# Low-rank update on one core: ScalarE's spreads as hardware loops, GpSimd narrowing whole groups, one wait a turn on VectorE

## The chip, the core and the metric

The kernel runs on one core of a Trainium2 chip. The core has five engines with an instruction stream each: PE (TensorE, matrix products), DVE (VectorE), ACT (ScalarE), POOL (GpSimd) and SP (SyncE), which here only issues transfers. They share a scratch memory of 128 partitions (SBUF). PE writes its products into PSUM. Sixteen DMA engines move data between the chip's memory (DRAM) and SBUF. The engines synchronise by semaphores: an instruction can wait until a semaphore has reached a value, and add to one when it is done.

The metric is the device time of one execution in microseconds. The kernel before takes 123.73 us, the median of three runs from 123.73 to 123.92.

## The reference

```python
batch, seq, d_model, r = 16, 512, 768, 16
lora = np.matmul(np.matmul(x, A), B)        # A is 768 x 16, B is 16 x 768
return (x + scale * lora).astype(np.float32)
```

`x` has 8192 rows of 768 floats, 25.2 MB, and the result has the same size. The inner matrices are small: per row 16 numbers `y = x A` are made, and from those the update `y B`.

## The kernel before

The 8192 rows are 64 tiles of 128 rows, and all of `x` stays in SBUF (`x_all`, fp32), where the update is added in place. The tiles are cut into five parts of 8, 16, 16, 12 and 12 tiles (`PARTS`); a part is loaded by one or two DMAs (eight loads, `LOADS`, numbered 0 to 7) and stored by one (five stores, 0 to 4). All are issued by the Sync engine in order. Loads 0 to 5 go out early. Load 6 (tiles 52 to 59) waits until the first products are out, since its place holds temporaries before. Load 7 (tiles 60 to 63) waits for the sums of parts 0 and 1 (`summed(0)`, `summed(1)`, in program order) and for `s_taken` to reach 8, since its place holds narrowed data (`xn_a`). Stores 0 and 1 wait for load 6 to have landed, and each later store for the last sum of its part.

The work goes in 16 groups of four tiles, numbered 0 to 15. For each group:

1. *Narrowing*, `narrowed` (line 221): fp32 to fp16. ScalarE does two of the tiles and GpSimd the other two. The target is `xn_a` for groups 0 to 7 (two tiles at the end of `x_all`, not yet loaded), `xt` for groups 8 to 10 (`PLACE`, in which the transpose then works in place), and `xn_c` for groups 11 to 15 (the first two tiles of `x_all`, free once store 0 has landed, semaphore `s_out0`).
2. *Transpose*, `turned` (line 277): VectorE transposes 32x32 blocks into `xt`.
3. *Projection*, `projected` (line 312): PE multiplies `xt` by a block-diagonal copy of `A` (`w_bd`) in 24 matmuls into `y_ps[h]`, where `h` is the group's parity. The second matmul raises `s_taken` (narrowed space read out of, since the transpose is done), the last raises `s_y`.
4. *Spread*, `on_scalar` (line 263): ScalarE scales `y` and writes it in four `mul`s, one for each block of 32 partitions, to the diagonal blocks of `y_bd[h]`; the last raises `s_spread[h]`.
5. *Raise*, `raised` (line 333): PE multiplies `y_bd[h]` by `B` into `lora[p]`, two tiles at a time (p is 0 or 1), when VectorE has freed that space (`s_free`).
6. *Sum*, `summed` (line 282): VectorE adds `lora[p]` to the two tiles.

VectorE's order is written out: in turn t it transposes group t, and then does the two sums of group t - 2. Before each transpose it waits for `s_y` (the projection of group t - 1 is done, so `xt` may be overwritten; this wait is a separate instruction or stands beside it, line 298) and for both narrowed halves (`s_narrow`). PE runs a hardware loop (`Fori`) of eight passes with two groups each: projection of a group, then the raises of the group before. ScalarE's program is written out: for each group the spread, then its half of the narrowing of group g + 2. GpSimd narrows group by group.

Narrowing of group g waits for its load, and for `s_taken` to reach g (groups 1 to 7, 12 to 15), for `s_y` to reach g (8 to 10), or for store 0 (11). The block-diagonal `w_bd` is made at the start by four copies of `w_one`: three on GpSimd (lines 247 and 250, with a wait after each) and the fourth on VectorE (line 292).

Of the kernel before, what the change touches and what calls it, by code (L numbers as in the profile page):

```python
# [16 lines left out]
GROUP = 4  # L17

SUB = 2
# [4 lines left out]
PLACE = range(8, 11)  # L24
# [7 lines left out]
def kernel(  # L32
# [11 lines left out]
    Q = 32  # L44
    NQ = P // Q
# [4 lines left out]
    R = A.shape[1]  # L50
    NC = D // 64
    NG = sum(PARTS) // GROUP
    PAIRS = GROUP // 2
    assert sum(PARTS) * P == T and NG * GROUP == sum(PARTS)
    sc = float(scale)


    def sb(name, shape, dtype):
        return nc.alloc_sbuf_tensor(name, shape, dtype).ap()

    def ps(name, shape):
        return nc.alloc_psum_tensor(name, shape, fp32).ap()
# [3 lines left out]
    ROOM = sum(PARTS)  # L66
    x_all = sb("x_sb", [P, ROOM, D], fp32)
    w_bd = sb("w_bd", [P, NC, 2, P], MM_DT)
    b_mm = sb("b_mm", [P, D], MM_DT)
    xt = sb("xt", [P, GROUP, D], MM_DT)  # L70
    y_bd = sb("y_bd", [P, 2, GROUP, P], MM_DT)
    lora = [ps(f"lora_ps{i}", [P, 2, D]) for i in range(2)]
    y_ps = [ps(f"ps_yt{i}", [P, GROUP, Q]) for i in range(2)]
# [17 lines left out]
    w_one = lent(NC * 2 * R, MM_DT)[0:Q].rearrange("i (c k r) -> i c k r", c=NC, k=2)  # L91

    def narrow_in(t):
        v = x_all[:, ds(t, SUB), :].rearrange("p s d -> p (s d)").bitcast(MM_DT)
        return v.rearrange("p (s d) -> p s d", s=GROUP)

    xn_a, xn_c = narrow_in(ROOM - SUB), narrow_in(0)

    def narrow_of(g):
        return xn_a if g < PLACE[0] else xt if g in PLACE else xn_c  # L100

    sems = []

    def sem(name):
        sems.append(nc.alloc_semaphore(name))
        return sems[-1]
# [32 lines left out]
    s_wv = sem("s_wv")  # L139
    s_w, s_bh, s_bp, s_bm = sem("s_w"), sem("s_bh"), sem("s_bp"), sem("s_bm")  # L140
    s_first, s_taken = sem("s_first"), sem("s_taken")
    s_narrow = [sem(f"s_narrow{h}") for h in range(2)]
    s_turned = [sem(f"s_turned{h}") for h in range(2)]
    s_y, s_lora = sem("s_y"), sem("s_lora")
    s_spread = [sem(f"s_spread{h}") for h in range(2)]


# [61 lines left out]
    def narrowed(e, copy, g, first, n=SUB):  # L209
        t = g * GROUP + first  # L210
        for k in dict.fromkeys(load_of(t + k) for k in range(n)):
            if (e, k) not in here:
                here.add((e, k))
                e.wait_ge(s_load[k], 16)
        if g in PLACE:
            e.wait_ge(s_y, g)
        elif g == PLACE[-1] + 1:
            e.wait_ge(s_out0, 16)
        elif g:
            e.wait_ge(s_taken, g)  # L220
        ins = copy(out=narrow_of(g)[:, ds(first, n), :], in_=tiles(t, n))  # L221

        ins.then_inc(s_narrow[g % 2] if g else s_first if first else s_a, 1)

    def on_gpsimd(e):
        e.memset(a_rows[0:Q], 0.0).then_inc(s_ready, 1)  # L226
        e.memset(b_rows, 0.0).then_inc(s_brows, 1)
        e.memset(pick, 0.0).then_inc(s_pick, 1)
        e.memset(w_bd.rearrange("p c k m -> p (c k m)").bitcast(fp32), 0.0)  # L229
        e.memset(y_bd.rearrange("p h s m -> p (h s m)").bitcast(fp32), 0.0).then_inc(s_ready, 1)  # L230
        e.wait_ge(s_pick, 1)
        e.affine_select(
            out=pick, in_=pick, compare_op=mybir.AluOpType.not_equal, fill=1.0, base=0,
            pattern=[[0, NQ], [-APART, Q]], channel_multiplier=1,
        ).then_inc(s_pick, 1)
        narrowed(e, e.tensor_copy, 0, 0)
        e.wait_ge(s_pick, 2)
        e.wait_ge(s_b, 16)
        e.tensor_copy(out=b_half, in_=b_rows).then_inc(s_bh, 1)  # L239
        e.wait_ge(s_ready, 3)  # L240
        e.tensor_copy(  # L241
            out=w_one.rearrange("i (c e) k r -> i c e (k r)", c=SETS),
            in_=a_t[0:Q].rearrange("i k r (e c) -> i c e (k r)", c=SET)[:, 0:SETS, 0:SET, :],
        ).then_inc(s_w, 1)
        e.wait_ge(s_w, 1)
        for b in range(NQ - 1):
            e.tensor_copy(  # L247
                out=w_bd[ds(b * Q, Q), :, :, ds(b * Q, R)], in_=w_one
            ).then_inc(s_w, 1)
            e.wait_ge(s_w, b + 2)  # L250
        for g in range(1, NG):
            narrowed(e, e.tensor_copy, g, SUB)

    def on_scalar(e):
        narrowed(e, e.copy, 0, SUB)
        e.wait_ge(s_bp, 1)
        e.copy(out=b_mm, in_=lora[0][:, 0, :]).then_inc(s_bm, 1)  # L257
        narrowed(e, e.copy, 1, 0)
        for g in range(NG):
            e.wait_ge(s_y, g + 1)  # L260
            for b in range(NQ):
                q = ds(b * Q, Q)
                last = e.mul(out=y_bd[q, g % 2, :, q], in_=y_ps[g % 2][q, :, :], mul=sc)  # L263
            last.then_inc(s_spread[g % 2], 1)
            if g + 2 < NG:
                narrowed(e, e.copy, g + 2, 0)

    def on_vector(e):
        e.wait_ge(s_a, SETS * 16 + 1)
        e.transpose(  # L270
            out=a_t[0:Q].rearrange("i k r c -> i (k r) c"),
            in_=a_rows[0:Q].rearrange("c (i k r) -> c (k r) i", k=2, r=R),
        ).then_inc(s_ready, 1)

        def turned(g):
            ts = [v.bitcast(fp32) for v in (xt, narrow_of(g))]
            e.transpose(out=ts[0], in_=ts[1]).then_inc(s_turned[g % 2], 1)  # L277

        def summed(g, p):
            xs = tiles(g * GROUP + 2 * p, 2)  # L280
            e.wait_ge(s_lora, (g + 1) * PAIRS + p + 1)
            ins = e.tensor_tensor(out=xs, in0=xs, in1=lora[p % 2], op=mybir.AluOpType.add)  # L282
            if p + 1 == PAIRS and g in STORED:
                ins.then_inc(s_sum, 1)
            elif g + 1 < NG:
                ins.then_inc(s_free[g % 2][p], 1)

        e.wait_ge(s_first, 1)
        turned(0)
        b = NQ - 1  # L290
        e.wait_ge(s_w, 1)
        e.tensor_copy(
            out=w_bd[ds(b * Q, Q), :, :, ds(b * Q, R)], in_=w_one
        ).then_inc(s_wv, 1)
        for t in range(1, NG + 2):
            if t < NG:
                e.wait_ge(s_y, t)
                e.wait_ge(s_narrow[t % 2], 2 * ((t + 1) // 2))  # L298
                turned(t)
            if t > 1:  # L300
                for p in range(PAIRS):
                    summed(t - 2, p)

    def on_tensor(e):


        def projected(h):
            xv = xt.rearrange("p s (c j k) -> p s c j k", c=NC, k=2)
            e.wait_ge(s_turned[h], 1)
            for m in range(MMS):  # L310
                c, k = divmod(m, 2)
                mm = e.matmul(  # L312
                    y_ps[h], w_bd[:, c, k, :], xv[:, :, c, :, k],
                    start=(m == 0), stop=(m == MMS - 1),
                )
                if m == 0:
                    mm.then_inc(s_turned[h], -1)
                if m == 1:

                    mm.then_inc(s_taken, 1)  # L320
                if m == MMS - 1:
                    mm.then_inc(s_y, 1)

        def raised(h, p):
            if p == 0:
                e.wait_ge(s_spread[h], 1)
            free = s_free[1 - h][p]
            e.wait_ge(free, 1)
            t = lora[p % 2]
            mms = []  # L330
            for k in range(2):
                for n0, w in ((0, 512), (512, 256)) if k == 0 else ((0, 256), (256, 512)):
                    mms.append(e.matmul(  # L333
                        t[:, k, ds(n0, w)], y_bd[:, h, 2 * p + k, :], b_mm[:, ds(n0, w)],
                        start=True, stop=True,
                    ))
            if p == 0:
                mms[2].then_inc(s_spread[h], -1)
            mms[1].then_inc(free, -1)
            mms[-1].then_inc(s_lora, 1)  # L340

        e.wait_ge(s_pick, 2)
        e.wait_ge(s_bh, 1)
        for n0, w in ((0, 512), (512, 256)):
            last = e.matmul(  # L345
                lora[0][:, 0, ds(n0, w)], pick.rearrange("p b r -> p (b r)"),
                b_half[:, ds(n0, w)], start=True, stop=True,
            )
        last.then_inc(s_bp, 1)
        e.wait_ge(s_w, NQ)  # L350
        e.wait_ge(s_wv, 1)
        e.wait_ge(s_bm, 1)

        with e.Fori(0, NG // 2):
            for h in range(2):
                projected(h)
                for p in range(PAIRS):
                    raised(1 - h, p)
        for p in range(PAIRS):
            raised(1, p)  # L360
# [50 lines left out]
```

## Time and profile before

| | |
|---|---|
| median of three runs | 123.73 us |
| the profiled execution | 123.87 us |
| its span, first to last instruction | 122.1 us |
| PE busy (522 matmuls) | 56.6 us |
| VectorE busy | 82.8 us |
| ScalarE busy | 42.8 us |
| GpSimd busy | 30.7 us |
| bytes moved | 50.45 MB, on average 413 GB/s |

The profile is taken by the hardware in one execution. Times in it count from the start of the span. A row of the timeline has the start, the duration, the engine, the line and the tile written and read, and in brackets how long the engine was idle before it and who ended that. Rows of stretches have, after the stretch and its length, the busy time and the number of instructions of PE, its weight loads, VectorE, ScalarE and GpSimd, and then PE's granted clock (1.00 is full), the mean busy share of the 16 DMA engines, and GB/s. Of the DMA queues, q1 carries the kernel's transfers, and q14 fetches instructions. An issue's row has the size and the time from issue to landing.

### The profile page before, as it was taken

What the parts mean: (1) busy time and instruction counts of PE and PEld (TensorE: products, weight loads), DVE (VectorE), ACT (ScalarE), POOL (GpSimd) and SP (SyncE); (2) the same over time, 40 slices, a digit from 0 to 9 for tenths busy, and PEclk for the clock granted to TensorE, in tenths of its full rate; (3) what the DMA queues carried; (4) which work ended last, traced back from release to release, by engine and by line L of the source; (5) the groups of instructions that cost most, each with busy time, mean ns of one, the idle gap of its engine ahead of it and who ended that gap; (6) DMA issues with size and microseconds to landing.
All of it is one profiled execution on the core that took longest, in us unless ns stands there. A gap on an engine that the chain in (4) does not pass through costs nothing.

```text
span 122.1 us, 1371 instructions
## 1 busy us (share of the span) xinstructions
PE 56.6 (46%) x522; PEld 37.0 (30%) x522; DVE 82.8 (68%) x50; ACT 42.8 (35%) x82; POOL 30.7 (25%) x31
## 2 busy tenths in 40 slices
PE   0000278775764766737694608876475740000000
PEld 0000075453351542514464208444154320000000
DVE  0002905599999999999969649999999998000000
ACT  4003344782652735265252084474380300000000
POOL 7722660441340422224040044034040000000000
PEclk9999999999999999999859995899999999655555
DMA  3999999998998989999999999799799799899980
GB/s 60 421 441 439 443 419 435 435 548 370 403 515 379 459 387 399 439 395 427 431 431 467 430 499 467 322 515 467 306 515 483 305 495 423 387 423 507 423 387 36
DMA packets 1930, 50.45 MB, mean 413 GB/s; under 512 B 236, under 2 KB 236, under 8 KB 392
## 3 DMA queue, kind: packets, MB, share of 16 engines
q1 hardware_dynamic: 1928, 50.43, 96.7%
q14 instruction: 2, 0.02, 0.0%
HBM read 25.26 MB, written 25.17 MB: 413 GB/s over the span
## 4 chain that ended last, share of the span: by engine, by line
DMA 45%; DVE 25%; issue 5%; PE 4%; POOL 4%; SPq 1%; POOLq 0%; DVEq 0%
DMA x_sb<-in_x_dram 29%; DVE x_sb L282 15%; DMA out_dram<-x_sb 9%; DVE xt L277 9%; DMA x_sb<-in_A_dram 6%; PE ps_yt L312 3%; DVE x_sb L270 2%; POOL w_bd L247 1%; POOL x_sb L221 1%; SPq L181 1%; POOL x_sb L226 1%; POOL x_sb L241 1%; PE lora_ps L333 1%; POOLq L406 0%; DVEq L298 0%
## 5 line engine op out<-in xcount | busy, mean ns | idle before, releaser
L282 DVE TENSOR_TENSOR x_sb<-x_sb,lora_ps 128x1536 f32<-128x1536 f32 x32 | 54.0, 1730 | 0.0
L312 PE MATMUL ps_yt<-xt,w_bd 128*128 128x128 f16 x384 | 27.8, 233 | 19.7 <-DVE xt L277 17.0
L333 PE MATMUL lora_ps<-b_mm,y_bd 128*128 128x512 f16 (+1 forms) x136 | 28.7, 340 | 12.2 <-DVE x_sb L282 8.6
L312 PEld LDWEIGHTS ps_yt<-xt,w_bd 128*128 128x128 f16 x384 | 25.2, 103 | 25.7 <-issue 25.7
L221 ACT CAST x_sb<-x_sb 128x1536 f16<-128x1536 f32 x13 | 19.1, 1472 | 35.9 <-PE ps_yt L312 18.9
L221 POOL CAST x_sb<-x_sb 128x1536 f16<-128x1536 f32 x13 | 19.1, 1468 | 40.3 <-PE ps_yt L312 29.2
L277 DVE STREAM_TRANSPOSE xt<-x_sb 128x1536 f32<-128x1536 f32 x13 | 22.9, 1763 | 8.3 <-POOL x_sb L221 4.8
L333 PEld LDWEIGHTS lora_ps<-b_mm,y_bd 128*128 128x128 f16 x136 | 11.8, 102 | 25.3 <-DVE x_sb L282 11.7
L263 ACT ACTIVATE y_bd<-ps_yt 32x128 f16<-32x128 f32 x64 | 17.2, 268 | 6.2 <-PE ps_yt L312 5.3
L270 DVE STREAM_TRANSPOSE x_sb<-x_sb 32x1024 f32<-32x1024 f32 x1 | 1.9, 1941 | 11.3 <-DMA x_sb<-in_A_dram 11.3
L221 ACT CAST xt<-x_sb 128x1536 f16<-128x1536 f32 x3 | 4.4, 1472 | 9.6 <-PE ps_yt L312 9.6
L221 POOL CAST xt<-x_sb 128x1536 f16<-128x1536 f32 x3 | 4.4, 1469 | 13.0 <-PE ps_yt L312 13.0
L345 PE MATMUL lora_ps<-x_sb 128*128 128x512 f16 (+1 forms) x2 | 0.8, 500 | 12.6 <-POOL x_sb L239 12.6
L277 DVE STREAM_TRANSPOSE xt<-xt 128x1536 f32<-128x1536 f32 x3 | 5.3, 1778 | 1.1 <-POOL xt L221 1.0
L345 PEld LDWEIGHTS lora_ps<-x_sb 128*128 128x128 f16 x2 | 0.1, 104 | 12.5 <-issue 12.5
L239 POOL CAST x_sb<-x_sb 128x768 f16<-128x768 f32 x1 | 0.8, 829 | 4.6 <-DMA x_sb<-in_B_dram 4.6
L221 ACT ACT_TABLE_LOAD x1 | 1.3, 1283 | 0.9 <-SPq L159 0.9
L247 POOL COPY w_bd<-x_sb 32x384 f16<-32x384 f16 x3 | 1.5, 501 | 0.2
L229 POOL MEMSET w_bd<- 128x1536 f32 x1 | 1.4, 1373 | 0.0
L257 ACT CAST b_mm<-lora_ps 128x768 f16<-128x768 f32 x1 | 0.8, 799 | 0.8 <-PE lora_ps L345 0.8
L226 POOL MEMSET x_sb<- 32x1024 f32 x1 | 0.9, 942 | 0.5 <-SPq L159 0.5
L241 POOL CAST x_sb<-x_sb 32x384 f16<-32x384 f32 x1 | 0.8, 829 | 0.9 <-DVE x_sb L270 0.9
(9 smaller groups left out, 2.6 us busy)
## 6 DMA issues: line engine op xcount, KB each, us to landing
out_dram<-x_sb SPq DMA_DIRECT2D x2, 6144.0 KB, 24.0
x_sb<-in_x_dram SPq DMA_DIRECT2D x3, 3072.0 KB, 20.7
out_dram<-x_sb SPq DMA_DIRECT2D x2, 4608.0 KB, 18.0
x_sb<-in_x_dram SPq DMA_DIRECT2D x1, 6144.0 KB, 34.8
x_sb<-in_x_dram SPq DMA_DIRECT2D x1, 4608.0 KB, 45.2
out_dram<-x_sb SPq DMA_DIRECT2D x1, 3072.0 KB, 11.4
x_sb<-in_x_dram SPq DMA_DIRECT2D x1, 2304.0 KB, 9.6
x_sb<-in_x_dram SPq DMA_DIRECT2D x1, 1536.0 KB, 9.5
```

The source lines that it names most:

```text
L181: e.dma_start(out=a_rows[c : SET * SET : SET, :], in_=blocks[ds(c * SET, SET), :]).then_inc(s_a, 16)
L221: ins = copy(out=narrow_of(g)[:, ds(first, n), :], in_=tiles(t, n))
L226: e.memset(a_rows[0:Q], 0.0).then_inc(s_ready, 1)
L229: e.memset(w_bd.rearrange("p c k m -> p (c k m)").bitcast(fp32), 0.0)
L241: e.tensor_copy(out=w_one.rearrange("i (c e) k r -> i c e (k r)", c=SETS), in_=a_t[0:Q].rearrange("i k r (e c) -> i c e (k r)", c=SET)[:, ...
L247: e.tensor_copy(out=w_bd[ds(b * Q, Q), :, :, ds(b * Q, R)], in_=w_one).then_inc(s_w, 1)
L263: last = e.mul(out=y_bd[q, g % 2, :, q], in_=y_ps[g % 2][q, :, :], mul=sc)
L270: e.transpose(out=a_t[0:Q].rearrange("i k r c -> i (k r) c"), in_=a_rows[0:Q].rearrange("c (i k r) -> c (k r) i", k=2, r=R),).then_inc(s_r ...
L277: e.transpose(out=ts[0], in_=ts[1]).then_inc(s_turned[g % 2], 1)
L282: ins = e.tensor_tensor(out=xs, in0=xs, in1=lora[p % 2], op=mybir.AluOpType.add)
L312: mm = e.matmul(y_ps[h], w_bd[:, c, k, :], xv[:, :, c, :, k], start=(m == 0), stop=(m == MMS - 1),)
L333: mms.append(e.matmul(t[:, k, ds(n0, w)], y_bd[:, h, 2 * p + k, :], b_mm[:, ds(n0, w)], start=True, stop=True,))
```

## The change

- Each group outside 8 to 10 is narrowed by GpSimd alone, four tiles in one instruction, into one of two spaces by the group's parity (`xn_a[h]`, `xn_c[h]`, two tiles each). It waits for `s_taken` to reach g - 1 in place of g. Of group 0, and of groups 8 to 10, ScalarE still narrows half.
- `s_y` becomes a pair by parity. ScalarE's spread waits for `s_y[h]` to be 1, and its second `mul` takes the 1 away. Its third `mul` raises `s_narrow[1 - h]`, by which VectorE's next transpose is released.
- ScalarE runs two hardware loops of three passes with two spreads each (groups 0 to 5, 10 to 15), and between them the spreads of groups 6 to 9 and the narrowings of 8 to 10 are written out. The narrowing of group g there stands ahead of the spread of group g - 1.
- Narrowing of groups 8 to 10 waits for the new `s_raise`, which the first matmul of each raise (p = 0) increments.
- VectorE no longer waits for `s_y`. Its one wait per turn is for `s_narrow`, to which the spread's count is added.
- The fourth copy to `w_bd` moves from VectorE to ScalarE, behind `b_mm`; GpSimd's waits between its three copies become one after them.

```diff
-    xn_a, xn_c = narrow_in(ROOM - SUB), narrow_in(0)
+    xn_a = [narrow_in(ROOM - GROUP + SUB * h) for h in range(2)]
+    xn_c = [narrow_in(SUB * h) for h in range(2)]
...
-        return xn_a if g < PLACE[0] else xt if g in PLACE else xn_c
+        return xn_a[g % 2] if g < PLACE[0] else xt if g in PLACE else xn_c[g % 2]
...
-    s_y, s_lora = sem("s_y"), sem("s_lora")
+    s_y = [sem(f"s_y{h}") for h in range(2)]
+    s_raise, s_lora = sem("s_raise"), sem("s_lora")
...
         if g in PLACE:
-            e.wait_ge(s_y, g)
+            e.wait_ge(s_raise, g)
         elif g == PLACE[-1] + 1:
             e.wait_ge(s_out0, 16)
-        elif g:
-            e.wait_ge(s_taken, g)
+        elif g > 1:
+            e.wait_ge(s_taken, g - 1)
...
-            e.wait_ge(s_w, b + 2)
+        e.wait_ge(s_w, NQ)
         for g in range(1, NG):
-            narrowed(e, e.tensor_copy, g, SUB)
+            if g in PLACE:
+                narrowed(e, e.tensor_copy, g, SUB)
+            else:
+                narrowed(e, e.tensor_copy, g, 0, GROUP)
...
-        narrowed(e, e.copy, 1, 0)
-        for g in range(NG):
-            e.wait_ge(s_y, g + 1)
+        b = NQ - 1
+        e.wait_ge(s_w, 1)
+        e.copy(out=w_bd[ds(b * Q, Q), :, :, ds(b * Q, R)], in_=w_one).then_inc(s_wv, 1)
+
+        def spread(h):
+            e.wait_ge(s_y[h], 1)
             for b in range(NQ):
                 q = ds(b * Q, Q)
-                last = e.mul(out=y_bd[q, g % 2, :, q], in_=y_ps[g % 2][q, :, :], mul=sc)
-            last.then_inc(s_spread[g % 2], 1)
-            if g + 2 < NG:
-                narrowed(e, e.copy, g + 2, 0)
+                ins = e.mul(out=y_bd[q, h, :, q], in_=y_ps[h][q, :, :], mul=sc)
+                if b == 1:
+                    ins.then_inc(s_y[h], -1)
+                if b == 2:
+
+                    ins.then_inc(s_narrow[1 - h], 1)
+            ins.then_inc(s_spread[h], 1)
+
+        def rounds(n):
+            with e.Fori(0, n):
+                for h in range(2):
+                    spread(h)
+
+        assert PLACE[0] % 2 == 0 and len(PLACE) == 3
+        rounds(PLACE[0] // 2 - 1)
+        spread(0)
+        for g in PLACE:
+            narrowed(e, e.copy, g, 0)
+            spread((g - 1) % 2)
+        rounds((NG - PLACE[-1]) // 2)
...
-        b = NQ - 1
-        e.wait_ge(s_w, 1)
-        e.tensor_copy(
-            out=w_bd[ds(b * Q, Q), :, :, ds(b * Q, R)], in_=w_one
-        ).then_inc(s_wv, 1)
+
+        count = [0, 0]
         for t in range(1, NG + 2):
             if t < NG:
-                e.wait_ge(s_y, t)
-                e.wait_ge(s_narrow[t % 2], 2 * ((t + 1) // 2))
+                count[t % 2] += 3 if t in PLACE else 2
+                e.wait_ge(s_narrow[t % 2], count[t % 2])
                 turned(t)
...
-                    mm.then_inc(s_y, 1)
+                    mm.then_inc(s_y[h], 1)
...
             if p == 0:
+                mms[0].then_inc(s_raise, 1)
                 mms[2].then_inc(s_spread[h], -1)
```

## The prediction

> **What bounds the kernel now.** I read the page's head first, then the DMA's share by stretches, then the Sync engine's row in the timeline.
>
> ```profile
> span 122.1 us, 1371 instructions
> PE 56.6 (46%) x522; PEld 37.0 (30%) x522; DVE 82.8 (68%) x50; ACT 42.8 (35%) x82; POOL 30.7 (25%) x31
> q1 hardware_dynamic: 1928, 50.43, 96.7%
> q14 instruction: 2, 0.02, 0.0%
> ...
> 2.00:60.00 58.00, 30.34 (x294) 19.96 (x295) 43.05 (x27) 25.38 (x48) 20.65 (x20) 1.00 1.00 425
> 60.00:118.40 58.40, 26.21 (x232) 17.04 (x229) 39.73 (x24) 16.35 (x34) 8.81 (x6) 0.82 1.02 438
> ...
> 0.97 0.85 SPq L164 DMA_DIRECT2D x_sb<-in_x_dram  x2
> 58.69 45.11 SPq L174 DMA_DIRECT2D out_dram<-x_sb  x5
> ...
> 76.92 26.87 SPq L174 DMA_DIRECT2D out_dram<-x_sb  x3
> ```
>
> No compute engine is busy for more than 68% of the span, but the sixteen DMA engines are: their share (the column before the last) is 1.00 from 2 to 60 us and 1.02 from there to 118.4 us (a little over one, since a transfer is counted where it starts). The first load is issued at 0.97, data moves from about 2 us, and then the engines never run dry until the end. So the end moves only if a DMA is issued so late that the engines before it run out of work, or if the bytes on the slowest of the sixteen change.
>
> How much lateness that allows is seen from the issues. One row each, asked for in a window around the issue: load 7 (52.84), store 2 (76.92, the row above), store 3 (a window of 91.6 to 91.9), store 4.
>
> ```profile
> 52.84 0.33 SPq L164 DMA_DIRECT2D x_sb<-in_x_dram  x1
> ...
> x_sb<-in_x_dram SPq DMA_DIRECT2D x1, 1536.0 KB, 9.5
> out_dram<-x_sb SPq DMA_DIRECT2D x1, 6144.0 KB, 22.5
> out_dram<-x_sb SPq DMA_DIRECT2D x1, 4608.0 KB, 18.4
> out_dram<-x_sb SPq DMA_DIRECT2D x1, 4608.0 KB, 17.7
> ...
> 22.96 35.71 DMA x_sb<-in_x_dram
> ```
>
> Store 3 lands at 91.75 + 18.4 = 110.15. Store 4 is issued at 58.69 + 45.11 - 0.33 = 103.47 and lands at 121.2. Data follows an issue by about 1 us (0.97 to 2). So store 4 may be late by 110.15 - 103.47 - 1.0 = 5.7 us before the last engine idles, and by about 4.8 us before the first fourteen or so do (they finish some 0.9 us ahead, below). For store 3 the sum is the same: store 2 lands at 76.9 + 22.5 = 99.4, less 91.75, less 1.0, is 6.6. Load 7 follows load 6, which lands at 22.96 + 35.71 = 58.67: 58.67 - 52.84 - 1.0 = 4.8.
>
> Now the tail. These are four answers of the DMA view: the windows 83 to 84.4, 97.4 to 99 and 118 to 122 us, each in forty slices, and then 66.8 to 68 and 96 to 97 for the queue's row.
>
> ```profile
> GB/s 0 0 0 0 1404 4213 1404 1404 4213 0 0 0 1404 1404 0 1405 1404 0 1405 1404 0 0 0 0 0 0 0 0 0 0 0 0 1404 0 0 0 0 0 0 0
> ...
> GB/s 0 0 0 0 0 0 922 2765 922 922 2765 0 0 922 922 0 1843 0 0 0 0 0 0 0 0 0 0 0 0 0 0 922 0 0 922 0 0 922 0 0
> ...
> GB/s 737 1475 1106 737 737 0 0 0 0 0 369 0 369 369 0 0 0 0 0 0 0 0 0 0 0 0 0 0 0 0 0 0 0 0 0 0 0 0 0 0
> ...
> q14 instruction: 1, 0.01, 1.6%
> ...
> q14 instruction: 1, 0.01, 1.9%
> ```
>
> In each of the first three, the unit (1404, 922, 369) is one packet of a store on one DMA engine. At 83 us fifteen engines begin store 2 within 0.55 us and one comes 0.45 us after them. At 97.6 us thirteen begin store 3 together and three come 0.6 to 0.8 us later. At the end thirteen start their last packet between 118.0 and 118.5, and three at 119.0, 119.2 and 119.3. The packets are equal, so the kernel ends 0.8 us after thirteen of its engines. Between the even start and this lie two instruction fetches, one at 66.8 to 68 us and one at 96 to 97 us, each on one engine. That is two fetches for three late engines: the third is unaccounted for.
>
> **The change part by part.** Prices are rows of the timeline.
>
> ```profile
> 16.06 2.73 PE ps_yt L312 x24
> 18.81 1.11 ACT L263 ACTIVATE y_bd<-ps_yt 32x128 f16<-32x128 f32 x4 [0.87 <-PE ps_yt L312]
> 18.81 1.78 DVE L277 STREAM_TRANSPOSE xt<-x_sb 128x1536 f32<-128x1536 f32 x1 [3.43 <-PE ps_yt L312]
> 22.72 1.78 DVE L277 STREAM_TRANSPOSE xt<-x_sb 128x1536 f32<-128x1536 f32 x1 [2.13 <-POOL x_sb L221]
> ...
> 47.68 1.76 DVE L277 STREAM_TRANSPOSE xt<-x_sb 128x1536 f32<-128x1536 f32 x1
> 49.36 3.38 DVE L282 TENSOR_TENSOR x_sb<-x_sb,lora_ps 128x1536 f32<-128x1536 f32 x2
> 49.59 1.54 PE L312 MATMUL ps_yt<-xt,w_bd 128*128 128x128 f16 x24 [0.95 <-DVE xt L277]
> 51.16 1.47 ACT L221 CAST xt<-x_sb 128x1536 f16<-128x1536 f32 x1 [3.64 <-PE ps_yt L312]
> 51.22 0.81 PE L333 MATMUL lora_ps<-b_mm,y_bd 128*128 128x512 f16 x4
> 52.66 1.11 ACT L263 ACTIVATE y_bd<-ps_yt 32x128 f16<-32x128 f32 x4
> 52.77 1.78 DVE L277 STREAM_TRANSPOSE xt<-xt 128x1536 f32<-128x1536 f32 x1
> ...
> 70.17 1.47 POOL L221 CAST x_sb<-x_sb 128x1536 f16<-128x1536 f32 x1 [6.31 <-DMA out_dram<-x_sb]
> 71.74 1.78 DVE L277 STREAM_TRANSPOSE xt<-x_sb 128x1536 f32<-128x1536 f32 x1 [2.69 <-POOL x_sb L221]
> 73.67 2.63 PE L312 MATMUL ps_yt<-xt,w_bd 128*128 128x128 f16 x24 [3.74 <-DVE xt L277]
> ```
>
> 1. *VectorE waits for ScalarE's third spread instead of for the projection.* The projection ends 1.91 + 1.54 us after a transpose starts; ScalarE's third of four `mul`s ends 3/4 of 1.11 = 0.83 later, with about 0.1 for two hand-overs: the next transpose can start 4.4 us after the last. VectorE itself needs 4.99 (one transpose and two sums), so in steady turns this costs nothing; the cover is 0.6 us. At the start there is none: group 1 goes from 18.81 to 16.06 + 2.73 + 0.03 + 0.83 + 0.1 = 19.75, and group 2 to 19.75 + 4.4 = 24.15 against 22.72. Lag 1.4 us, kept through the first eight groups.
>
> 2. *GpSimd narrows whole groups into two spaces.* A whole group costs it 2 x 1.47 = 2.94 us in place of 1.47 on two engines, below 4.99, and with two spaces it may begin a turn earlier. Hidden, except where a group is narrowed on demand: group 11 waits for store 0, which lands at 70.1. There it is ready at 70.17 + 2.94 = 73.1, not 71.65.
>
> 3. *Groups 8 to 10, narrowed into `xt` on both engines.* The wait becomes the first matmul of the raise, some 0.45 us after the projection's end, and ScalarE narrows (1.47) before it spreads, so VectorE's new wait ends last: 1.91 + 1.54 + 0.45 + 1.47 + 0.83 + 0.2 = 6.4 us a turn against 5.1. Lags: 1.4 + 1.3 = 2.7 at group 8, 4.0 at 9, 4.3 at 10 (68.2 against 63.96, where the old kernel lost a microsecond to a slow clock). Queued behind VectorE's wait are the two sums of the group two turns back, which PE's raise and the Sync engine wait for. Load 7 goes out behind the sum of group 5, late by 1.4 of the 4.8 allowed.
>
> 4. *Group 11 resets the lag.* VectorE is free at 68.2 + 5.0 = 73.2, GpSimd ready at 73.15: the transpose starts at 73.25, not 71.74. Lag 1.5. If PE's clock is low (the 2.63 us row), a turn there takes 1.91 + 2.63 + 0.93 = 5.5, so 0.5 more per such turn and up to 1.1 in each turn of point 3. I take 2.5 us of lag at the end, with 1.5 and 4.7 as ends. Store 4 is then issued at 106, inside the 4.8 allowed: no cost.
>
> 5. *`w_bd`'s last quarter moves from VectorE to ScalarE* behind `b_mm`; VectorE's copy took 0.45 us, and GpSimd's three take longer than both. Nothing, and GpSimd's waits between its copies (0.05 each) are saved: at most 0.1, into a lag that is hidden.
>
> 6. *Fewer stored instructions.*
>
> ```profile
> L298 DVEq EVENT_SEMAPHORE  x15: 21/21/21, 18.1 to 90.6; - x15
> ...
> L263 ACT ACTIVATE y_bd<-ps_yt 32x128 f16<-32x128 f32 x64 | 17.2, 268 | 6.2 <-PE ps_yt L312 5.3
> L354 PEldq COMPARE_BRANCH  x8: 76/208/227, 21.7 to 96.9; - x8
> ```
>
> ScalarE's 64 `mul`s become 32 in its program (two loops of two spreads, four spreads written out), and 12 of its 16 narrowings go: 82 working instructions become 39, with a handful for loops. VectorE loses the 15 separate waits of line 298 and one copy, out of 65. GpSimd, with 31, stays the same; PE already loops. The trace does not say whose the two fetches are, but the longest straight programs are those two. If both fall away, the end falls back to the thirteen: -0.8. If only one does, or the unexplained third engine stays late, between 0 and -0.3. I take -0.6.
>
> Sum: starting from the profiled execution's 123.87, 0 for points 1 to 5 and -0.6 gives 123.3; the median of the runs is 0.14 lower, so 123.1 us. Something below 0.2%, 0.25 us, can't be told from no change here.
>
> [...] PE's loop takes eight branches in this trace and the span holds two fetches, so the trace shows no fetch for each pass of a loop of its size; ScalarE's loop is far shorter.
>
> **Rivals.**
>
> *A. Bound by the bytes, nothing moves.* The fetches stay (other engines', or one more page for the loops), or the third late engine sets the end as before. For it: three late engines and only two fetches. Time 123.7 (123.5 to 123.95).
>
> *B. The turns of groups 8 to 11 run cold, and store 4 comes too late: slower.* PE idles longer in point 3's turns.
>
> ```profile
> 59.00:71.00 12.00, 7.64 (x64) 5.21 (x64) 9.04 (x6) 3.41 (x6) 2.30 (x2) 0.86 1.11 475
> 71.00:79.00 8.00, 4.79 (x39) 3.72 (x39) 7.26 (x5) 4.23 (x10) 2.10 (x2) 0.79 0.92 399
> 85.00:95.00 10.00, 6.37 (x68) 4.05 (x65) 10.00 (x7) 4.05 (x10) 1.93 (x2) 1.00 1.05 452
> ```
>
> The granted clock (third from the end) is already 0.86 and 0.79 there, against 1.00 in steady turns. It decides once the lag exceeds 4.8 us: all three turns cold (4.0 at group 11) and two or three cold turns after it at 0.5 each give 5.0 to 5.5, and each further one half a microsecond. Time 124.2, at six cold turns more 125. Against it: 85 to 95 shows the steady turns warm. [...]
>
> [...]
>
> **How the numbers follow.** Likeliest 0.50: cover holds, fetches fall away, 123.1 (122.8 to 123.48). A 0.28. B 0.12, C 0.04, something unforeseen and slower 0.06. The range reaches from 122.8 to 124.2: it leaves out gains beyond the thirteen engines (0.06) and the far parts of B and C (0.1). Faster 0.50, same 0.28, slower 0.22.
>
> **What would show it.** Right: the DMA share stays at 1.00 from 2 us; q14 has no packet in the span; the last packets start within half a microsecond; store 4 is issued near 106; VectorE's row at group 8 begins near 55.4 and at group 11 near 73.3; L298 is gone. Wrong: a slice after 100 us with a low DMA share (B); more packets on q14 (C); the same three late engines with none on q14 (A).

## The result and the profile after

The changed kernel takes 124.72 us, the median of four runs from 124.52 to 124.99, against 123.75 before: a ratio of 1.0077, with an interval from 1.0056 to 1.0098. It is slower by about 0.97 us, where 0.6 us of gain had been forecast. The profiled execution took 124.99 us, and its span is 122.5 us.

These two numbers hold the answer already. The span of the changed kernel lies between 122.2 and 122.5 us in its four runs; that of the old one lay between 122.0 and 122.5 in forty runs taken later (in three sets, with medians of 122.1 to 122.2). The time around the span, time less span, was 1.76 to 1.86 us in those runs of the old kernel and is 2.22, 2.46, 2.49 and 2.49 us now, 0.66 us more by the medians of the table below (2.48 and 1.82). So about 0.3 of the 0.97 us are inside the span, and as the old kernel took 123.89 to 124.00 us in those later sets, 0.14 to 0.25 above its 123.75 here, much of that may be scatter between sets. Most of the loss lies where the timeline shows no instruction of the kernel.

The head of the page, the queue, and the same stretches as before:

```profile
span 122.5 us, 1354 instructions
...
PE 56.9 (46%) x522; PEld 37.3 (30%) x522; DVE 82.2 (67%) x49; ACT 25.7 (21%) x71; POOL 46.0 (38%) x31
...
q1 hardware_dynamic: 1928, 50.43, 96.2%
...
2.00:60.00 58.00, 29.52 (x283) 20.34 (x284) 39.97 (x24) 13.06 (x37) 28.10 (x19) 0.97 1.00 426
60.00:118.40 58.40, 27.36 (x241) 16.92 (x239) 42.27 (x26) 11.54 (x34) 16.68 (x7) 0.85 1.01 436
```

The DMA engines are as full as before (1.00 and 1.01). The row of q14 is gone from the page: both instruction fetches have left the span. Everything that was to be hidden was hidden.

VectorE's transposes in the timeline (not its sums), with PE's projections of groups 8 and 9, one of GpSimd's narrowings of four tiles and the Sync engine's stores:

```profile
19.71 1.78 DVE L301 STREAM_TRANSPOSE xt<-x_sb 128x1536 f32<-128x1536 f32 x1 [4.79 <-ACT y_bd L271]
24.08 1.78 DVE L301 STREAM_TRANSPOSE xt<-x_sb 128x1536 f32<-128x1536 f32 x1 [2.60 <-ACT y_bd L271]
...
55.43 1.78 DVE L301 STREAM_TRANSPOSE xt<-xt 128x1536 f32<-128x1536 f32 x1 [1.32 <-ACT y_bd L271]
57.35 2.72 PE L333 MATMUL ps_yt<-xt,w_bd 128*128 128x128 f16 x24 [2.33 <-DVE xt L301]
62.73 1.78 DVE L301 STREAM_TRANSPOSE xt<-xt 128x1536 f32<-128x1536 f32 x1 [2.21 <-ACT y_bd L271]
64.65 2.72 PE L333 MATMUL ps_yt<-xt,w_bd 128*128 128x128 f16 x24 [3.25 <-DVE xt L301]
70.26 1.78 DVE L301 STREAM_TRANSPOSE xt<-xt 128x1536 f32<-128x1536 f32 x1 [2.45 <-ACT y_bd L271]
...
75.27 1.76 DVE L301 STREAM_TRANSPOSE xt<-x_sb 128x1536 f32<-128x1536 f32 x1
77.58 2.75 POOL L223 CAST x_sb<-x_sb 128x3072 f16<-128x3072 f32 x1 [2.31 <-PE ps_yt L333]
...
58.69 48.61 SPq L176 DMA_DIRECT2D out_dram<-x_sb  x5
```

VectorE now waits for ScalarE's spread at the start and in groups 8 to 10 (the brackets name line 271). It is 3.5 us behind the old kernel from group 11 on (75.27 against 71.74), and store 4 is issued at 58.69 + 48.61 - 0.33 = 106.97 instead of 103.47. Store 3 still keeps the DMA engines full then.

Now the tail, in the DMA view of 118 to 122 us, and that of 121 to 127 us, which reaches past the span, each in forty slices:

```profile
GB/s 1106 0 369 1475 737 0 1106 369 0 0 0 0 0 0 0 0 369 0 0 0 0 0 0 0 0 0 0 0 0 0 0 0 0 0 0 0 0 0 0 0
...
GB/s 0 0 0 0 0 0 0 0 0 0 0 0 0 0 0 0 0 0 0 0 0 0 0 0 0 55 0 0 0 0 0 0 0 0 0 0 0 0 0 0
...
q14 instruction: 1, 0.01, 0.5%
```

In the first row a single engine starts its last packet late, at 119.6 us, 0.9 us behind the rest, where three did before. In the second, the one packet, at slice 25 (124.75 us), is an instruction fetch, 2.3 us after the last instruction of the kernel. Its share of 0.5% of the sixteen engines over 6 us makes 0.48 us. The old kernel's trace has no packet there; its view of the same window says:

```profile
DMA packets 0, 0.00 MB, mean 0 GB/s; under 512 B 0, under 2 KB 0, under 8 KB 0
```

### The profile page after: what moved, and what is told of

The parts are those of the page before. It is cut to its first block, busy times and chain, and to the rows that moved or that the text cites. A ratio compares the mean times of both kernels' runs of the same rounds, so it can differ in the third digit from the quotient of the medians.

```text
span 122.5 us, 1354 instructions
## 1 busy us (share of the span) xinstructions
PE 56.9 (46%) x522; PEld 37.3 (30%) x522; DVE 82.2 (67%) x49; ACT 25.7 (21%) x71; POOL 46.0 (38%) x31
## 4 chain that ended last, share of the span: by engine, by line
DVE 58%; PE 10%; DMA 6%; ACT 6%; issue 3%; POOL 3%; SPq 1%; ACTq 0%; POOLq 0%
DVE x_sb L306 35%; DVE xt L301 21%; PE ps_yt L333 9%; DMA x_sb<-in_A_dram 6%; ACT y_bd L271 3%; ACT xt L223 3%; DVE x_sb L294 2%; POOL w_bd L249 1%; SPq L183 1%; PE lora_ps L354 1%; POOL x_sb L228 1%; POOL x_sb L243 1%; ACTq L280 0%; ACTq L218 0%; POOLq L428 0%
## 5 line engine op out<-in xcount | busy, mean ns | idle before, releaser
L223 POOL CAST x_sb<-x_sb 128x3072 f16<-128x3072 f32 (+1 forms) x13 | 34.4, 2650 | 18.7 <-PE ps_yt L333 11.2
L223 ACT CAST x_sb<-x_sb 128x1536 f16<-128x1536 f32 x1 | 1.5, 1472 | 8.8 <-DMA x_sb<-in_x_dram 8.8
```

## The experiments

From this came **theory F**: the change shortens the stored programs, so that an engine's fetch of its next instructions no longer falls in mid-span, where the transfers cover it, but behind the last store, where nothing does. Against it stood **theory T** (VectorE's lag spreads the end of the sixteen DMA engines inside the span) and later **theory L** (ScalarE's loops cost something of their own at the end). The table has all runs; the paragraphs take them in turn. Sizes are those of the compiled programs in bytes, 64 to an instruction (e2's 15 more instructions on VectorE make 5376 bytes of 4416). The two loops on ScalarE also make the programs of VectorE and GpSimd four instructions longer (4160 bytes without them in e1, 4416 with them). Spans are on record to 0.1 us, and only packets of 8 KB on q14 (55 GB/s in a slice of 0.15 us) are counted as fetches. The experiments ran in three sets, each on a chip of its own: e1 to e4, e5 to e8, and e9. The row of the old kernel is from runs beside the second set; beside the first it took 123.91, beside the last 124.00. Its time less span is 1.81 or 1.82 in all three, which is why time less span is compared across sets.

| kernel | ScalarE | VectorE | GpSimd | fetches in the span, at us | behind it | span, us | time less span, median | time, us |
|---|---|---|---|---|---|---|---|---|
| before | 6656 | 5184 | 4160 | 67.3, 96.4 | none | 122.0-122.3 | 1.82 | 123.89 |
| after | 4288 | 4416 | 4416 | none | 124.75 | 122.2-122.5 | 2.48 | 124.72 |
| e1 | 5696 | 4160 | 4160 | 73.0 | none | 122.0-122.5 | 1.82 | 123.97 |
| e2 | 4288 | 5376 | 4416 | 98.2 | none seen | 122.3-122.6 | 2.16 | 124.51 |
| e3 | 4288 | 4416 | 5056 | none | 123.07, 124.87 | 122.0-122.3 | 3.03 | 125.24 |
| e4 | 5696 | 5120 | 4800 | 73.0, 98.3 | 123.38 | 122.2-122.5 | 2.28 | 124.62 |
| e5 | 5696 | 4416 | 4160 | 70.8 | 123.82 | 122.1-122.3 | 2.25 | 124.35 |
| e6 | 5696 | 4160 | 4416 | 72.8 | none | 122.0-122.4 | 1.80 | 124.00 |
| e7 | 4288 | 5376 | 5824 | 90.9, 98.0 | none seen | 122.1-122.4 | 2.14 | 124.47 |
| e8 | 5696 | 4288 | 4160 | 72.7 | 124.93 | 122.2-123.1 | 2.13 | 124.96 |
| e9 | 6208 | 5376 | 4416 | 57.4, 98.0 | none | 122.1-122.5 | 1.81 | 124.02 |

**e1: ScalarE's loops written out.**

```diff
-            with e.Fori(0, n):
+            for _ in range(n):
                 for h in range(2):
                     spread(h)
```

> Theory F (fetch at the end): the changed kernel's 124.7 us against 123.75 lies mostly outside its span (time less span 2.2 to 2.5 us, against 1.8 before), since an engine's stored program now ends so short that its next instruction fetch falls behind the last store instead of beside the transfers. Written out again, ScalarE's program is longer by some 22 instructions and its fetch falls inside the span: if ScalarE's was the late one, or the two loops of ScalarE lengthen the other programs too, time less span goes back to 1.8 and the time to 123.8 to 124.1, with one fetch in the span on q14; if the late fetch is VectorE's or GpSimd's alone, 124.5 to 124.9 stays. Theory T (tail inside the span): VectorE's lag of 3.5 us spreads the sixteen engines at the end; the loops have no part in it, and the time stays at 124.5 to 124.9 whatever the loops are.

The time is 123.97 us (ratio to the old kernel 1.001, 0.9998 to 1.0022), time less span 1.82. One fetch lies in the span, in the view of 70 to 75 us:

```profile
q14 instruction: 1, 0.01, 0.4%
```

Theory T falls: VectorE's order and waits are those of the changed kernel, its last store is issued even later than there (107.8 us against 106.97), and the loss is gone. Since writing the loops out changes three programs at once (ScalarE's from 4288 to 5696 bytes, VectorE's and GpSimd's from 4416 to 4160), the run does not say whose fetch it was.

**e2: 15 met waits on VectorE.**

```diff
                 count[t % 2] += 3 if t in PLACE else 2
+                e.wait_ge(s_taken, t)
```

> One wait more per turn on VectorE, on a semaphore that is there already when VectorE comes to it, so no turn gets longer; its program gets 15 instructions longer, as it was before the change. Theory F: if the fetch behind the span is VectorE's, it moves into the span, time less span goes back to 1.8 and the time to 123.8 to 124.1; otherwise 124.5 to 124.9. Theory T: 124.5 to 124.9.

124.51 us (1.0054, 1.0036 to 1.0072). VectorE's fetch is in the span again, at 98.2 us, and time less span fell from 2.48 to 2.16, but not to 1.8. I had expected all or nothing. Part of it was VectorE's; something else remained.

**e3: 20 met waits on GpSimd** (after its three copies to `w_bd`).

```diff
         e.wait_ge(s_w, NQ)
+        for _ in range(20):
+            e.wait_ge(s_pick, 2)
```

> Twenty waits that are met already ahead of GpSimd's second narrowing, where GpSimd has time. Theory F: if the fetch behind the span is GpSimd's, time less span goes back to 1.8 and the time to 123.8 to 124.1; otherwise 124.5 to 124.9. Theory T: 124.5 to 124.9.

A miss the other way: 125.24 us (1.0109, 1.0092 to 1.0126), time less span 3.03, and the span no longer. The view of 121 to 127 us shows two fetches behind the span where the changed kernel has one:

```profile
GB/s 0 0 0 0 0 0 0 0 0 0 0 0 0 55 0 0 0 0 0 0 0 0 0 0 0 55 0 0 0 0 0 0 0 0 0 0 0 0 0 0
...
q14 instruction: 2, 0.02, 1.1%
```

The edit is GpSimd's alone, ten instructions (4416 to 5056 bytes), so the second fetch is read as its own. The run costs 0.55 us (3.03 against 2.48) for no work at all, and fits neither T nor L.

**e4: e1, e2 and e3 together.**

> The three together: ScalarE's loops written out, VectorE's 15 extra waits, GpSimd's 20. Theory F, whichever engine it was: time less span 1.8, two or three fetches inside the span, time 123.7 to 124.1. Theory T: 124.5 to 124.9, and time less span still 2.2 to 2.5.

124.62 us (1.0056, 1.0039 to 1.0073), not the 1.8 us around the span that theory F was to give: the fetches read as ScalarE's and VectorE's are inside (73.0 and 98.3, by e1's 73.0 and e2's 98.2), but GpSimd's padding goes with one behind the span (123.38), as in e3. The miss is the padding's: it had made a late engine of one that was not.

**e5 and e6: e1, with VectorE's or GpSimd's program back at the 4416 bytes of the changed kernel.** Eight met waits (which become four instructions) ahead of VectorE's second transpose, or after GpSimd's copies:

```diff
+        for _ in range(8):
+            e.wait_ge(s_a, SETS * 16 + 1)
         count = [0, 0]
```

> ScalarE's loops written out (that kernel took 123.97 us, time less span 1.8), and eight waits already met ahead of VectorE's second transpose, which bring VectorE's compiled program from 4160 back to the 4416 bytes it has in the changed kernel; GpSimd's stays at 4160. Theory F with VectorE as an engine whose fetch falls behind the span: time less span 2.2 to 2.5, time 124.4 to 124.7, a fetch on q14 behind the span and none of VectorE's inside. Theory F with GpSimd or ScalarE alone: 1.8 and 123.8 to 124.2. Theory L (a loop on ScalarE itself costs time at the end of the execution): 1.8, as ScalarE has no loop here.

> The same with the eight waits on GpSimd: its program has the 4416 bytes of the changed kernel, VectorE's stays at 4160. Theory F with GpSimd as the late engine: time less span 2.2 to 2.5, time 124.4 to 124.7. Theory F with VectorE or ScalarE alone: 1.8 and 123.8 to 124.2. Theory L: 1.8.

e5 takes 124.35 us (1.0042, 1.0026 to 1.0059; a shade under the 124.4 expected), e6 124.00 (1.0011, 1.0002 to 1.0021). e1 and e5 differ in VectorE's eight waits alone: they cost 2.25 - 1.82 = 0.43 us, none of it in the span. The view of 121 to 127 us of e5:

```profile
GB/s 0 0 0 0 0 0 0 0 0 0 0 0 0 0 0 0 0 0 55 0 0 0 0 0 0 0 0 0 0 0 0 0 0 0 0 0 0 0 0 0
...
q14 instruction: 1, 0.01, 0.5%
```

So VectorE is one late engine of the changed kernel, and GpSimd's 4416 bytes cost nothing. e6, in the same set as e5, has the eight waits on GpSimd instead and stays at 1.80.

**e7: the whole change, with VectorE (15 instructions) and GpSimd (22) made longer.** The edits of e2 and e3, the latter with 44 waits.

> The whole change with its loops, and VectorE's 15 and GpSimd's 22 instructions of met waits more (5376 and 5824 bytes), so that the fetches of both should fall inside the span. ScalarE's program stays at 4288. Theory F, if only VectorE and GpSimd were late: time less span 1.8 and time 123.8 to 124.2, two fetches inside the span. Theory F, if ScalarE's 4288 bytes fetch behind the span as well, or if GpSimd's fetch still does: 2.2 to 2.5. Theory L: 2.2 to 2.5, as the loops are there.

124.47 us (1.0039, 1.0024 to 1.0053), time less span 2.14, just under the 2.2 expected if ScalarE is late. Both fetches are inside the span, at 90.9 and 98.0. So 0.32 us are ScalarE's, by a fetch behind the span (the record shows none) or by its loops: F and L were still both open.

**e9: the whole change with its loops; e2's waits, and 30 instructions on ScalarE ahead of the loops.**

```diff
         narrowed(e, e.copy, 0, SUB)
+        for _ in range(60):
+            e.wait_ge(s_load[0], 16)
         e.wait_ge(s_bp, 1)
```

> The whole change with both loops; VectorE's 15 waits as in the run of its own, and some 30 instructions of met waits on ScalarE ahead of its loops, where it idles (6208 bytes in place of 4288). GpSimd stays as the change has it. Theory F (an instruction fetch behind the span is the whole cost, VectorE's and ScalarE's): both fetches fall inside the span, time less span 1.8, time 123.8 to 124.1, the same as before the change. Theory L (the loops themselves cost at the end): time less span stays at 2.1 to 2.2 and the time at 124.3 to 124.6.

124.02 us against 124.00 for the old kernel in the same runs (1.0004, 0.9992 to 1.0015), time less span 1.81. The page's queue row:

```profile
q14 instruction: 2, 0.02, 0.0%
```

e2 and e9 differ in ScalarE's met waits alone, and 30 more instructions make the kernel 0.35 us faster around the span. Theory L falls: both loops are there. Every other part of the change is there too, so the parts that move work cost nothing together; nor do the programs of PE and SyncE, which e9 leaves as they are in the changed kernel.

That ScalarE's cost is a fetch as VectorE's is, is not shown. The one packet behind the span of the changed kernel is missing in e2, where VectorE's fetch is inside, so it is read as VectorE's. It starts 1.7 us after the span's end in e5, where ScalarE's program is long, 2.3 us after it in the changed kernel, and 2.8 us after it in e3, where GpSimd's fetch comes too. So something of about half a microsecond (2.3 less 1.7, an estimate) lies ahead of it when ScalarE's program is short, but no packet of it is on record.

**e8: how much lateness the stores bear.** e1, with two more transposes on VectorE ahead of its last two sums.

```diff
+            if t == NG + 1:
+                w = w_bd.rearrange("p c k m -> p (c k m)").bitcast(fp32)
+                e.wait_ge(s_lora, (t - 1) * PAIRS + 1)
+                for v in (xt, xn_c[0]):
+                    e.transpose(out=v.bitcast(fp32).rearrange("p s d -> p (s d)"), in_=w)
             if t > 1:
```

> ScalarE's loops written out, and two more transposes of 1.76 us on VectorE ahead of its last two sums (into space that is no longer needed), so that store 4 is issued some 3.5 us later, near 110.4 us instead of 106.9. By the prediction's sum (4.8 us of lateness until thirteen engines run dry, 5.7 until the last; the lag is 3.5 already) the sixteen engines run dry from 109 to 110.3 us until 111.4, and the span grows by 1.0 to 2.3 us, to 123.2 to 124.5. If the lag were not hidden at all before, the span would grow by the whole 3.5.

The median span is 122.9 us (122.2 to 123.1) against 122.2 in e1. Sync's row and the stretch around the gap in the profiled run:

```profile
58.88 51.35 SPq L176 DMA_DIRECT2D out_dram<-x_sb  x5
...
108.00:112.00 4.00, 0.00 (x0) 0.00 (x0) 1.86 (x2) 0.00 (x0) 0.00 (x0) 0.50 0.39 166
112.00:118.00 6.00, 0.00 (x0) 0.00 (x0) 0.00 (x0) 0.00 (x0) 0.00 (x0) 0.50 1.15 492
```

Store 4 goes out at 58.88 + 51.35 - 0.33 = 109.9, 6.4 us later than in the old kernel, and now a hole shows (0.39 from 108 to 112 us). The span grew by 0.7, less than the 1.0 to 2.3 expected. That range took the lateness as 7.0 us; with the 6.4 us measured, the cover of 4.8 to 5.7 us gives 0.7 to 1.6, and the growth is at the lower end of it (in the profiled run, 123.1 against 122.1, it is 1.0). So the run agrees with the cover, toward its upper end. The changed kernel's 3.5 us lie well inside, and e1 has 4.3 us without a cost. (Time less span is 2.13 here, against 1.82 in e1: VectorE's program has 4288 bytes in place of 4160, and a fetch lies behind the span, at 124.93 us.)

## Why the prediction was wrong

*What bounds the kernel, and the cover.* Right. The share stayed at 1.00, the lag of 3.5 us cost nothing, and e8 found the edge where the sum put it. One figure of the sum is off: store 3's row stands at 91.89 us, not 91.75, which makes the cover 5.8 us in place of 5.7.

*Point 1.* Right: groups 1 and 2 at 19.71 and 24.08, for 19.75 and 24.15; steady turns at 4.99.

*Point 2.* The mechanism was right; four tiles at once take GpSimd 2.75 us, less than twice 1.47.

*Points 3 and 4.* Group 8 came at 55.43, for 55.4. Groups 9 and 10 came at 62.73 and 70.26, for 61.8 and 68.2, since PE's clock was low in both turns: the granted clock was 0.52 from 57.3 to 60.1 us and 0.50 from 64.6 to 67.4, where the two rows took 2.72 us, against 1.54 us for the same 24 matmuls at 72.19 us (1.00 from 72 to 78). PE's idle time before the two rows was 2.33 and 3.25 us, shorter than the 3.74 us before the old kernel's 2.63 us row, and it was 2.25 us before the row of 1.54: no idle time that sets the clock is shown. So the lag at group 11 is 3.5, for 1.5 to 2.5 and inside the ends given. Rival B's condition came half true: the granted clock over those turns is 0.68.

```profile
55.00:71.00 16.00, 9.35 (x65) 6.82 (x64) 10.90 (x7) 5.74 (x13) 4.20 (x3) 0.68 1.05 447
71.00:79.00 8.00, 4.90 (x57) 3.55 (x58) 8.00 (x6) 1.33 (x5) 5.65 (x3) 1.00 0.97 418
```

The clock was back before it could push the last store past its cover, so B's time did not come.

*Point 5.* Right: no cost shows.

*Point 6.* Here it failed, twice. First, "if both fall away, the end falls back to the thirteen: -0.8". Both fell away, and the span did not shrink: the 0.6 us of gain taken from this are missing in the result. Whose they were was guessed right: ScalarE's alone is long in e1 (73.0 us), VectorE's in e2 (98.2). But the third late engine, which the prediction noted and could not account for, still ends about a microsecond after the others, with no fetch in the span. The late engines are one more than the fetches in several traces, three for two (before, e9), two for one (e1), one for none (after, e3), and from 119 us on as many as the fetches in two others, two for two (e7) and one for one (e5). So more fetches mostly went with more late engines; that a fetch makes an engine late, as the prediction had it, was an estimate and is not shown, and the engine that is late without one sets the end all the same. Spans with two fetches (before, e9), one (e1, e6) or none (after, e3) can't be told apart: a fetch inside the span costs nothing here. In the span, rival A was right.

Second, and decisive, the sum took what lies around the span as fixed ("the median of the runs is 0.14 lower"). It grew by 0.66 us. No rival had this, and the packets of C did not come: q14 has none in the span. The shorter program did not only lose its fetch in the span: the one read as VectorE's lies at 96.4 us with 5184 bytes, and behind the last store, at 124.75, with 4416. By the pairs that differ in one engine's waits alone, VectorE's costs 0.43 us (e1 and e5) and ScalarE's 0.35 (e2 and e9): 0.78 one after the other, of which 0.66 show when both are late. Fetches at 57 to 98 us cost nothing: time less span is 1.80 to 1.82 in before, e1, e6 and e9, which have no other. With one or two behind the last store it is 2.13 to 3.03 (after, e3, e4, e5, e8). The 2.16 and 2.14 of e2 and e7 have no packet on record.

Open: what the engine that ends late without a fetch is held by; what ScalarE's 0.35 us are, since neither e2 nor e7 nor the changed kernel has a packet of its own for them (what is shown is that the length of its program decides); and what part of the span's 0 to 0.3 us of difference is more than scatter.

## What to carry to other kernels

Set the time less the span beside the span before anything else: where a loss lies around the span, no engine's row can explain it. When an edit changes the length of a program, ask where its instruction fetches will fall: in this kernel those beside the transfers (57 to 98 us) cost nothing, and at the lengths that did cost, one engine's program cost 0.3 to 0.55 us around the span. Padding with waits that are met already is a cheap test, and it can be a repair: the same 30 idle instructions that look like waste on ScalarE made the kernel 0.35 us faster. With that repair, and VectorE's, the change takes what the old kernel takes (124.02 us and 124.00), so it gains nothing either.

## What the runs showed of the hardware

- Without a change in the work, the length of one engine's program moved the time around the span in these runs: GpSimd at 4160 or 4416 bytes cost nothing (e1, e6: 1.82 and 1.80 us), at 4800 and 5056 about 0.5 us (e4, e3), and at 5824 a fetch is inside the span (e7, 90.9 us). VectorE at 4160 cost nothing (e1), at 4288 and 4416 some 0.3 to 0.45 (e8, e5), and at 5376 nothing (e9: 1.81).
- The two loops on ScalarE made the compiled programs of VectorE and GpSimd four instructions longer (4160 to 4416 bytes), and for VectorE that length costs 0.43 us (e1 and e5).
- One DMA engine starts its last packet at 119.6 us in the changed kernel's trace, 0.9 us behind the rest, though its queue shows no fetch in the span.
